# Hybrid decoder trunk: upper and lower weight parts share one tile, at places that depend on the block

## The chip, the cores and the metric

The kernel runs on one core of a Trainium2 chip. The metric is the device time of one execution in microseconds; lower is better. The time before is 1538.71 us, the median of three runs (1538.29 to 1539.51).

## The reference

One decoder layer over 256 tokens, with 16 learned meta tokens in front, in float32 with D_MODEL = 2048. Two branches are computed from one normalised input, gated, summed and projected; a squared-ReLU MLP follows.

```python
h = concatenate([meta, x], axis=1)                       # 272 columns
proj = rmsnorm(h, norm_mix_g) @ w_in                     # fq fk fv ff gq gk gv gr ga gate_fox gate_gla
o_fox = forgetting_attention(fq, fk, fv, ff, b_forget)   # 8 heads of 128
o_gla = gated_linear_attention(gq, gk, gv, g_log)        # 4 heads, keys 256, values 512
y = sigmoid(gate_fox) * (o_fox @ w_o_fox) + sigmoid(gate_gla) * (o_gla @ w_o_gla)
h = h + y @ w_out
h = h + square(relu(rmsnorm(h, norm_mlp_g) @ w_ff1)) @ w_ff2      # D_FF = 8192
return rmsnorm(h, final_norm_g)[:, N_META:]
```

## The kernel before

**How a product is made.** Activations lie transposed: 128 channels on the partitions, tokens along the row. A float32 value is held as an upper part, rounded to the type float32r that TensorE reads at full speed, and a lower part, the remainder. A product takes three terms: upper weights by upper and by lower activations, and lower weights by upper activations.

All weights stand in one DRAM array, w_all, in the order of their use (`stream()`): 272 blocks of 128 output channels by 2048 inputs. A block comes in two halves of 8 k-tiles (`weight_half`, L108). For each half SP issues one DMA of 512 KB into a tile raw (L118). ACT casts it to the upper part, whi (L120), and DVE subtracts to get the lower part, wlo (L121). Before, whi and wlo are two tags of the pool wp, each with five buffers of 4096 bytes a partition; raw has five too. The cast into a buffer waits until TensorE has read what stood in it.

**Two kinds of block.** `gemm2` (L154) serves blocks that need the 256 real tokens alone. For each of 16 k-tiles, mac2 issues one matmul with 512 columns (L143: upper weights by the upper and lower activations at once) and one with 256 (L144: lower weights by upper activations). Its result is evacuated by `total` or `add_residual`: ACT copies half the bank into a tile evb, and DVE adds. `gemm_all` (L163) serves the keys and values, which need the meta tokens too. For each k-tile, mac3 issues three matmuls with 272 columns: L148 (upper weights, lower activations x_lo), L150 (lower weights, x_hi) and L152 (upper weights, x_hi). There are 39 such blocks: 23 in the four GLA heads, 16 in the eight FoX heads. `join` and one DVE product evacuate them. The first seven blocks are computed while h still arrives (`first_weights`), and the small columns (`small`, L386) have weights of their own. Before every matmul TensorE loads its 128 columns of weights, while the matmul before is still reading its moving operand.

**How the moving operand is read.** `steps` (L135) views a row as (i a e) with a = e = 4 and has it read in the order a, i, e: four neighbouring elements (16 bytes), then 64 bytes on, until the row's end, and then again from the next 16 bytes.

**Where things lie.** x (L240) has rows of 576 elements, 2304 bytes or 9 times 256, and its data begin 16 elements into the tile. The other operands (og, y, x2, a) begin 32 elements into theirs (`operand`, L231), with k-tiles 2048 bytes apart; the weights of successive k-tiles are 512 bytes apart. In the built program every whi and wlo buffer begins 128 bytes past a multiple of 256. x_hi begins at 128 and x_lo at 192, and x, og, y, x2, a and of, as gemm2 reads them, at 192. So the moving operand stands 64 bytes from the weights in all 512/256 pairs, and in the 272s 64 (L148) or 0 (L150 and L152), modulo 256.

**Order.** Each engine's instructions are ordered by the tile framework's scheduler, which works from a timeline of its own; a changed wait or buffer can move neighbours past each other. Small work of the heads (scores, transposes, some of them fp32 matmuls) is put between blocks by `later`.

Of the kernel before, what the change touches and what calls it, by code (L numbers as in the profile page):

```python
# [7 lines left out]
F32 = mybir.dt.float32  # L8
F32R = mybir.dt.float32r
# [7 lines left out]
P = 128  # L17
D = 2048
KT = D // P
NM = 16  # L20
NT = 256
NA = NM + NT
EPS = 1e-6
FOX_H, FOX_D = 8, 128
# [8 lines left out]
NL = 4  # L33
# [32 lines left out]
def trunk(ctx: ExitStack, tc: tile.TileContext, hT, w_small, w_all, consts, w_alpha2, out):  # L66
# [3 lines left out]
    def nm(s):  # L70
        serial[0] += 1
        return f"{s}_{serial[0]}"

    const = ctx.enter_context(tc.tile_pool(name="const", bufs=1))
    keep = ctx.enter_context(tc.tile_pool(name="keep", bufs=1))
    wp = ctx.enter_context(tc.tile_pool(name="wp", bufs=5))
    tmp = ctx.enter_context(tc.tile_pool(name="tmp", bufs=2))
# [27 lines left out]
    chunk = [0]  # L105
    HK = KT // 2

    def weight_half(c, i, hi=None):  # L108

        raw = wp.tile([P, HK * P], F32, tag="raw", name=nm("raw"), bufs=RAW)  # L110
        if hi is None:
            hi = wp.tile([P, HK, P], F32R, tag="whi", name=nm("whi"))
        lo = wp.tile([P, HK, P], F32R, tag="wlo", name=nm("wlo"))

        def step(k0, n):
            k = slice(k0, k0 + n)
            cols = slice(k0 * P, (k0 + n) * P)
            nc.sync.dma_start(raw[:, cols], w_all[c][:, i * HK * P + cols.start : i * HK * P + cols.stop])  # L118
            r = raw.rearrange("p (k m) -> p k m", m=P)[:, k, :]
            nc.scalar.copy(hi[:, k, :], r)  # L120
            nc.vector.tensor_tensor(lo[:, k, :], r, hi[:, k, :].bitcast(F32), op=ALU.subtract)  # L121

        return hi, lo, step

    def next_weights(keep_hi=None):
        c = chunk[0]
        chunk[0] += 1
        parts = []
        for i in range(2):
            hi, lo, step = weight_half(c, i, None if keep_hi is None else keep_hi[:, HK * i : HK * (i + 1), :])  # L130
            step(0, HK)
            parts.append((hi, lo))
        return lambda k: (parts[k // HK][0][:, k % HK, :], parts[k // HK][1][:, k % HK, :])
# [43 lines left out]

    def total(ps, t=None):

        b = tmp.tile([P, NT], F32, tag="evb", name=nm("evb"))  # L180
        nc.scalar.copy(b, ps[:, NT:512])  # L181
        if t is None:
            t = tmp.tile([P, NT], F32, tag="evt", name=nm("evt"), bufs=4)
        nc.vector.tensor_tensor(t, ps[:, 0:NT], b, op=ALU.add)  # L184
        return t
# [45 lines left out]
    def operand(pool, name, nk=KT, at=0, **kw):  # L231

        t = pool.tile([P, at + nk * 2 * NT], F32R, name=nm(name), **kw)
        return t[:, at:].rearrange("p (k o t) -> p k o t", o=2, t=NT)
# [2 lines left out]
    h = keep.tile([P, KT, NA + 3], F32, name="h")  # L237

    ROW = 576
    x_row = keep.tile([P, 16 + KT * ROW + 48], F32R, tag="s1", name="x")[:, 16 : 16 + KT * ROW].rearrange(  # L240
        "p (k r) -> p k r", r=ROW)[:, :, 0 : 2 * NA]
    x_hi, x_lo = x_row[:, :, 0:NA], x_row[:, :, NA:]
    x = x_row[:, :, NM : NM + 2 * NT].rearrange("p k (o t) -> p k o t", t=NT)
# [33 lines left out]
    meta = take(KT, NM)  # L277

    def first_weights(c0, n, k0):
        raw = wp.tile([P, HK * P], F32, tag="raw", name=nm("raw"), bufs=RAW)  # L280
        hi = wp.tile([P, HK, P], F32R, tag="whi", name=nm("whi"))
        lo = wp.tile([P, HK, P], F32R, tag="wlo", name=nm("wlo"))
        r, hi, lo = (t[:, 0 : 2 * n * P].rearrange("p (c k m) -> p c k m", k=2, m=P)
                     for t in (raw, hi.rearrange("p k m -> p (k m)"), lo.rearrange("p k m -> p (k m)")))

        def load(c, m):
            return nc.sync.dma_start(r[:, c : c + m], w_all[c0 + c : c0 + c + m, :, k0 * P : (k0 + 2) * P].rearrange(
                "c p (k m) -> p c k m", m=P))

        def cut(c, m, ks=slice(0, 2)):  # L290
            cs = slice(c, c + m)
            i = nc.scalar.copy(hi[:, cs, ks], r[:, cs, ks])
            nc.vector.tensor_tensor(lo[:, cs, ks], r[:, cs, ks], hi[:, cs, ks].bitcast(F32), op=ALU.subtract)
            return i.ins

        return hi, lo, load, cut
# [31 lines left out]
    for s in range(KT // 2):  # L328
# [5 lines left out]
        for kk in range(2):  # L334
            k = 2 * s + kk
# [49 lines left out]

    small = []  # L386
    for i in range(2):
        w = wp.tile([P, HK, P], F32R, tag="whi", name=nm("whi"))
        nc.gpsimd.memset(w.bitcast(F32), 0.0)
        ws = wsm[:, HK * i : HK * (i + 1), :]  # L390
        nc.scalar.copy(w[:, :, 0:40], ws)
        nc.vector.tensor_tensor(w[:, :, 64:104], ws, w[:, :, 0:40].bitcast(F32), op=ALU.subtract)
        small.append(w)
# [71 lines left out]
    og_box = []  # L465

    def og_tile():
        if not og_box:
            og_box.append(operand(keep, "og", at=32, tag="s2"))
        return og_box[0]  # L470

    def gla_gates(ts):
# [30 lines left out]
    def gla_head(hd, sg, ready=None):  # L503
# [11 lines left out]
        def keys(i, ps):  # L515
            def four(ap):
                return ap.rearrange("p (g s t) -> p g s t", g=2, s=2)

            nc.vector.tensor_tensor(kx[:, i].rearrange("p g (s t) -> p g s t", t=C)[:, :, 0:3:2, :],
                                    four(ps[:, 0 : 4 * C]), four(en[:, i, 0 : 4 * C]), op=ALU.mult)  # L520
            nc.vector.tensor_tensor(kz[:, i], *(ap.unsqueeze(1).to_broadcast([P, 4, NB])
                                                for ap in (ps[:, 4 * C : NA], en[:, i, 4 * C :])), op=ALU.mult)

        if ready:
            ps = gemm_all(next_weights())
            keys(0, ready[1])
            keys(1, ps)
        else:
            for i in range(2):
                keys(i, gemm_all(next_weights()))  # L530
        for i in range(2):
            t = ready[0][:, i, :] if ready else total(gemm2(next_weights(), x))
            for q, n, at in ((0, Q1, 0), (Q1, Q3, NT)):
# [59 lines left out]
                nc.scalar.copy(vz, p2)  # L593

        for i in range(4):
            ps = gemm_all(next_weights())
            vT = tmp.tile([P, NA], F32, tag="vT", name=nm("vT"))
            nc.vector.tensor_tensor(vT, ps[:, 0:NA], rb, op=ALU.mult)
            nc.gpsimd.tensor_copy(vg[:, NB * i : NB * (i + 1)], vT[:, 4 * C :])
            later(1, lambda i=i, vT=vT: turn(i, vT))  # L600
# [57 lines left out]
    ps = bank(pg, "psa")  # L658
# [31 lines left out]
    cum.close()  # L690
    branches = ExitStack()
    late = branches.enter_context(tc.tile_pool(name="late", bufs=1, reuse_waits="tile"))
    of = operand(late, "of", FOX_H, at=0)
    negc = late.tile([P, FOX_H, NA], F32, name="negc")
    nc.gpsimd.dma_start(negc.rearrange("p h t -> p (h t)"), fdram.to_broadcast([P, FOX_H * NA]))
    fox = ExitStack()
# [16 lines left out]
    def fox_head(hd):  # L713
        fk = att.tile([P, NA], F32, tag="fk", name=nm("fk"))
        fq = att.tile([P, NT], F32, tag="fq", name=nm("fq"))
        ps = gemm_all(next_weights())
        nc.vector.tensor_tensor(fk, ps[:, 0:NA], rb, op=ALU.mult)
        t = total(gemm2(next_weights(), x))
        nc.vector.scalar_tensor_tensor(fq, t, FOX_D ** -0.5, rbt, op0=ALU.mult, op1=ALU.mult)
# [28 lines left out]
                nc.vector.tensor_scalar(pp, pp, st[:, 4 + b : 5 + b], None, op0=ALU.mult)  # L748

        later(1, scores)  # L750
        ps = gemm_all(next_weights())
        vT = tmp.tile([P, NA], F32, tag="vT", name=nm("vT"))
        nc.vector.tensor_tensor(vT, ps[:, 0:NA], rb, op=ALU.mult)
        va, pa = [], []
# [79 lines left out]
    for j0 in range(0, KT, 2):  # L834
# [5 lines left out]
        for j in range(2):  # L840
            t = total(gemm2(next_weights(), og))
            nc.vector.tensor_tensor(t, gates[2 * j + 1], t, op=ALU.mult)
            nc.vector.tensor_tensor(yf[:, j0 + j, :], gates[2 * j], t, op=ALU.add)
    y = operand(keep, "y", at=32, tag="s1")
    for j in range(KT):
        split_to(y[:, j, 0, :], y[:, j, 1, :], yf[:, j, :])
    mix.close()
# [3 lines left out]


    ht = h[:, :, NM:NA]
    x2 = operand(keep, "x2", at=32, tag="s2")

    def square_sum(j, acc):
        if j == 0:
# [4 lines left out]
            nc.gpsimd.tensor_tensor(acc, acc, sq, op=ALU.add)  # L862

    def add_residual(j, ps):
        b = tmp.tile([P, NT], F32, tag="evb", name=nm("evb"))
        nc.scalar.copy(b, ps[:, NT:512])
        nc.vector.tensor_tensor(ht[:, j, :], ps[:, 0:NT], ht[:, j, :], op=ALU.add)
        nc.vector.tensor_tensor(ht[:, j, :], ht[:, j, :], b, op=ALU.add)
# [22 lines left out]

    acc = gat.tile([P, NT], F32, tag="acc", name="acc3", bufs=1)
    for g in range(NG):
        a = operand(keep, "a", at=32, tag="s1")
        held = []
        for f in range(KT):
            ps = gemm2(next_weights(), x2, pool=px if g == 0 and f < 3 else pg)
            if g == 0 and f == 0:
                held.append(ps)
                continue  # L900
            if g == 0 and f == 1:
                relu2(a, 0, held.pop())
            relu2(a, f, ps)
        last = g == NG - 1
        for j in range(KT - NL if last else KT):
            add_residual(j, gemm2(next_weights(), a))
            if last:
                square_sum(j, acc)
                nc.scalar.activation(ht[:, j, :], ht[:, j, :], AF.Identity, scale=gain(2, j))
                if j == 0:  # L910
                    tc.keep_in_program_order(nc.scalar.preload_act_table_set("natural_log_exp_and_others"))


    whi = keep.tile([P, 48 + NL * KT * P + 16], F32R, tag="s2", name="whi_last")[:, 48 : 48 + NL * KT * P].rearrange(
        "p (n k m) -> p n k m", k=KT, m=P)
    ends = []
    for n in range(NL):
# [150 lines left out]
```

## Time and profile before

| | |
|---|---|
| median of 3 runs | 1538.71 us |
| the profiled execution | 1538.62 us, span 1536.8 us |
| granted TensorE clock | 0.999 |
| DVE busy / ACT busy | 1059.5 us (69%) / 789.6 us (51%) |
| DMA, mean over the span | 191 GB/s |

Four stretches follow each other, in us from the span's start: the first seven blocks (to 44), the GLA heads (to about 330), the FoX heads and first gates (to about 580), then branch projections, output projection and MLP (to the end). In a group's row stand line, engine, operation, output and inputs, shapes and count; then busy time, the mean ns of one, the idle time ahead, and what ended it. In a row of the timeline the first number is the start and the second the duration, in us. In a row of waits stand who waited for whom, us in total, times, and the longest. A matmul's duration runs until its results have left the array and so overlaps the next one's; the spacing of starts is what the stream costs.

### The profile page before, as it was taken

How to read it: one execution, taken by the hardware profiler on the slowest of the kernel's cores; microseconds unless marked ns; L12 is line 12 of the kernel's file. 1: busy time of each engine (PE TensorE's matmuls, PEld its weight loads, DVE VectorE, ACT ScalarE, POOL GpSimd, SP SyncE). 2: the span in 40 equal slices, each digit the busy share in tenths (PEclk: the TensorE clock that was granted, in tenths of full speed). 3: DMA queues.
4: the chain of work that ended last, by engine and by line, in shares of the span. 5: the costliest groups of instructions: out<-in, count | busy, mean ns of one | idle time of the engine just before them, and what ended most of it. 6: DMA issues, size and time to landing. Idle time of an engine off the chain costs nothing.

```text
span 1536.8 us, 25427 instructions
## 1 busy us (share of the span) xinstructions
PE 1525.6 (99%) x9812; PEld 1402.4 (91%) x9812; DVE 1059.5 (69%) x1659; ACT 789.6 (51%) x1271; POOL 127.6 (8%) x213
## 2 busy tenths in 40 slices
PE   9999999999999999999999999999999999999997
PEld 8999999999999999999999899999999999999997
DVE  7898858586666656556777876567765776667765
ACT  6766444555545444444655554445444454444563
POOL 6012000011100000000011000000000000000022
PEclk9999999999999999999999999999999999999999
DMA  9455545465555655666565556666565666656652
GB/s 325 165 165 165 182 161 188 157 210 173 167 166 182 201 195 199 197 198 200 182 212 195 193 195 201 195 200 196 194 202 196 201 196 197 199 195 201 192 192 101
DMA packets 86602, 293.09 MB, mean 191 GB/s; under 512 B 9112, under 2 KB 16800, under 8 KB 86352
## 3 DMA queue, kind: packets, MB, share of 16 engines
q1 hardware_dynamic: 85872, 289.62, 57.6%
q8 instruction: 77, 1.26, 0.3%
q0 software_dynamic: 176, 1.12, 0.2%
q10 hardware_dynamic: 432, 0.72, 0.1%
q14 instruction: 45, 0.37, 0.1%
HBM read 289.32 MB, written 2.11 MB: 190 GB/s over the span
## 4 chain that ended last, share of the span: by engine, by line
PE 97%; DVE 1%; ACT 1%; issue 0%; POOL 0%; DMA 0%; POOLq 0%; ACTq 0%; DVEq 0%
PE ps L143 51%; PE ps L144 26%; PE psa L152 5%; PE psa L148 5%; PE psa L150 4%; PE ps L359 1%; PE ps L361 1%; PE ps L937 1%; PE pa L557 1%; PE ps L921 0%; DVE wlo L121 0%; ACT whi L120 0%; PE po L620 0%; DMA h<-hT_dram 0%; POOL o L985 0%
## 5 line engine op out<-in xcount | busy, mean ns | idle before, releaser
L121 DVE TENSOR_TENSOR wlo<-raw,whi 128x1024 fp32r<-128x1024 f32 x522 | 640.3, 1227 | 400.0 <-ACT whi L120 390.8
L120 ACT CAST whi<-raw 128x1024 fp32r<-128x1024 f32 x522 | 546.9, 1048 | 604.7 <-PE ps L143 534.0
L143 PE MATMUL ps<-x,whi 128*128 128x512 f32 x1952 | 656.4, 382 | 0.8 <-DVE x L874 0.8
L144 PE MATMUL ps<-x,wlo 128*128 128x256 f32 x1952 | 535.3, 274 | 0.0
L143 PEld LDWEIGHTS ps<-x,whi 128*128 128x128 f32 x1952 | 366.4, 188 | 64.2 <-DVE x L874 1.1
L144 PEld LDWEIGHTS ps<-x,wlo 128*128 128x128 f32 x1952 | 366.4, 188 | 0.1
L143 PE MATMUL ps<-a,whi 128*128 128x512 f32 x960 | 320.0, 380 | 0.0
L144 PE MATMUL ps<-a,wlo 128*128 128x256 f32 x960 | 262.4, 274 | 0.0
L143 PEld LDWEIGHTS ps<-a,whi 128*128 128x128 f32 x960 | 179.9, 188 | 30.8
L148 PE MATMUL psa<-x,whi 128*128 128x272 f32 x640 | 182.5, 286 | 0.0
L152 PE MATMUL psa<-x,whi 128*128 128x272 f32 x640 | 180.8, 283 | 0.0
L144 PEld LDWEIGHTS ps<-a,wlo 128*128 128x128 f32 x960 | 180.2, 188 | 0.3
L150 PE MATMUL psa<-x,wlo 128*128 128x272 f32 x624 | 176.3, 283 | 0.0
L148 PEld LDWEIGHTS psa<-x,whi 128*128 128x128 f32 x640 | 120.0, 187 | 0.3
L152 PEld LDWEIGHTS psa<-x,whi 128*128 128x128 f32 x640 | 120.0, 187 | 0.0
L150 PEld LDWEIGHTS psa<-x,wlo 128*128 128x128 f32 x624 | 117.2, 188 | 0.0
L862 POOL TENSOR_TENSOR acc<-acc,hsq 128x256 f32<-128x256 f32 x26 | 28.4, 1092 | 736.4 <-ACT hsq L861 736.4
L143 PE MATMUL ps<-og,whi 128*128 128x512 f32 x256 | 85.8, 380 | 0.0
L143 PE MATMUL ps<-y,whi 128*128 128x512 f32 x256 | 85.3, 380 | 0.0
L144 PE MATMUL ps<-og,wlo 128*128 128x256 f32 x256 | 70.2, 274 | 0.0
L144 PE MATMUL ps<-y,wlo 128*128 128x256 f32 x256 | 70.0, 274 | 0.0
L184 DVE TENSOR_TENSOR evt<-ps,evb 128x256 f32<-128x256 f32 x158 | 65.9, 417 | 0.5 <-ACT evb L181 0.5
(297 smaller groups left out, 1420.9 us busy)
## 6 DMA issues: line engine op xcount, KB each, us to landing
raw<-w_all_dram SPq DMA_DIRECT2D x537, 512.0 KB, 4.3
raw<-w_all_dram SPq DMA_DIRECT2D x8, 384.0 KB, 6.7
h<-hT_dram SPq DMA_DIRECT2D x8, 275.0 KB, 6.8
negc<-fdram POOLq DMA_DIRECT2D x1, 1088.0 KB, 7.9
out_dram<-o SPq DMA_DIRECT2D x2, 512.0 KB, 2.6
raw<-w_all_dram SPq DMA_DIRECT2D x2, 256.0 KB, 3.7
room<-w_small_dram SPq DMA_DIRECT2D x1, 320.0 KB, 7.9
out_dram<-o ACTq DMA_DIRECT2D x1, 320.0 KB, 3.0
```

The costliest lines, as they stand in the source:

```text
L120: nc.scalar.copy(hi[:, k, :], r)
L121: nc.vector.tensor_tensor(lo[:, k, :], r, hi[:, k, :].bitcast(F32), op=ALU.subtract)
L143: nc.tensor.matmul(steps(ps), hi, steps(row(x)), start=first, stop=False)
L144: nc.tensor.matmul(steps(ps[:, 0:NT]), lo, steps(x[:, 0, :]), start=False, stop=last)
L148: nc.tensor.matmul(steps(ps[:, X_LO]), hi, steps(x_lo[:, k]), start=first, stop=False, skip_group_check=True)
L150: nc.tensor.matmul(steps(ps[:, 0:NA]), lo, steps(x_hi[:, k]), start=False, stop=last and hi is None, skip_group_check=True)
L152: nc.tensor.matmul(steps(ps[:, 0:NA]), hi, steps(x_hi[:, k]), start=False, stop=last, skip_group_check=True)
L184: nc.vector.tensor_tensor(t, ps[:, 0:NT], b, op=ALU.add)
L359: nc.tensor.matmul(steps(ps), hi, steps(row(x[:, k])), start=st, stop=False)
L361: nc.tensor.matmul(steps(ps[:, 0:NT]), lo, steps(x[:, k, 0]), start=False, stop=sp)
L557: nc.tensor.matmul(dst, k[:, a], q[:, a, :], start=(a == 0), stop=(a == 1))
L862: nc.gpsimd.tensor_tensor(acc, acc, sq, op=ALU.add)
```

## The change

The two tags whi and wlo become one tag w, of 2 x 1024 + 64 elements (8448 bytes, 33 times 256) with five buffers. A new function `pair` gives the two views. For a block without meta tokens the upper part begins at element 24 and the lower part 24 past the end of the upper one's 1024; for one with meta tokens (`meta=True`: keys, values, and the small columns) they begin at 0 and at 1024 + 20. To make room, evb has one buffer in place of two, and x loses its leading 16 elements. The offsets of the other operands move along, so that the 512/256 pairs keep their distance of 64 bytes.

```diff
+    def pair(meta=False):
+        n = HK * P
+        w = wp.tile([P, 2 * n + 64], F32R, tag="w", name=nm("w"))
+        a, b = (0, 20) if meta else (24, 24)
+        return [w[:, at : at + n].rearrange("p (k m) -> p k m", m=P) for at in (a, n + b)]
+
-    def weight_half(c, i, hi=None):
+    def weight_half(c, i, hi=None, meta=False):
         raw = wp.tile([P, HK * P], F32, tag="raw", name=nm("raw"), bufs=RAW)
+        upper, lo = pair(meta)
         if hi is None:
-            hi = wp.tile([P, HK, P], F32R, tag="whi", name=nm("whi"))
-        lo = wp.tile([P, HK, P], F32R, tag="wlo", name=nm("wlo"))
+            hi = upper
...
-        b = tmp.tile([P, NT], F32, tag="evb", name=nm("evb"))
+        b = tmp.tile([P, NT], F32, tag="evb", name=nm("evb"), bufs=1)
...
-    x_row = keep.tile([P, 16 + KT * ROW + 48], F32R, tag="s1", name="x")[:, 16 : 16 + KT * ROW].rearrange(
+    x_row = keep.tile([P, 0 + KT * ROW + 24], F32R, tag="s1", name="x")[:, 0 : 0 + KT * ROW].rearrange(
...
-        w = wp.tile([P, HK, P], F32R, tag="whi", name=nm("whi"))
+        w = pair(meta=True)[0]
...
-            og_box.append(operand(keep, "og", at=32, tag="s2"))
+            og_box.append(operand(keep, "og", at=56, tag="s2"))
...
-            ps = gemm_all(next_weights())
+            ps = gemm_all(next_weights(meta=True))
...
-    of = operand(late, "of", FOX_H, at=0)
+    of = operand(late, "of", FOX_H, at=24)
...
-    y = operand(keep, "y", at=32, tag="s1")
+    y = operand(keep, "y", at=16, tag="s1")
...
-    x2 = operand(keep, "x2", at=32, tag="s2")
+    x2 = operand(keep, "x2", at=56, tag="s2")
...
-        a = operand(keep, "a", at=32, tag="s1")
+        a = operand(keep, "a", at=16, tag="s1")
...
-    whi = keep.tile([P, 48 + NL * KT * P + 16], F32R, tag="s2", name="whi_last")[:, 48 : 48 + NL * KT * P].rearrange(
+    whi = keep.tile([P, 8 + NL * KT * P + 56], F32R, tag="s2", name="whi_last")[:, 8 : 8 + NL * KT * P].rearrange(
```

All gemm_all calls of the heads get `meta=True`; `add_residual` gets the same `bufs=1`, and `first_weights` takes its tiles from `pair()`.

In the built program x_hi now begins 64 bytes past a multiple of 256 and x_lo at 128. The weights of a block with meta tokens begin at 224 (upper) and 48 (lower): x_hi stands 96 bytes from the upper and 16 from the lower ones. Against the weights that are loaded while a matmul runs, which are the next matmul's, the distances are 80 (behind L148), 96 (L150) and 96 (L152). Weights of the other blocks begin at 64, their moving operands at 128.

The single buffer of evb moves instructions at the start of the GLA stretch. On ACT, behind the first seven blocks, six banks are evacuated (ps_85 to ps_90); join is the small copy for a bank with meta tokens. Before:

```order
L120 CAST whi_665<-raw_664 128x1024
L181 COPY evb_563<-ps_85 128x256
L181 COPY evb_567<-ps_86 128x256
L181 COPY evb_571<-ps_87 128x256
L120 CAST whi_671<-raw_670 128x1024
L181 COPY evb_575<-ps_88 128x256
L181 COPY evb_580<-ps_89 128x256
L120 CAST whi_772<-raw_771 128x1024
L175 COPY join_560<-ps_91 128x16
L181 COPY evb_583<-ps_90 128x256
```

And now:

```order
L126 CAST w_649<-raw_648 128x1024
L187 COPY evb_547<-ps_85 128x256
L126 CAST w_654<-raw_653 128x1024
L187 COPY evb_551<-ps_86 128x256
L181 COPY join_544<-ps_91 128x16
L126 CAST w_754<-raw_753 128x1024
L187 COPY evb_555<-ps_87 128x256
L126 CAST w_759<-raw_758 128x1024
L187 COPY evb_559<-ps_88 128x256
L181 COPY join_622<-psa_570 128x16
L126 CAST w_819<-raw_818 128x1024
L187 COPY evb_564<-ps_89 128x256
```

The copies no longer stand two and three in a row: a cast stands between any two, and the fifth bank (ps_89) is copied behind the fifth cast of this list in place of the second.

On PE, in the second block of values of the first GLA head, the two matmuls of the decays (pz) stand between the 272s. Before:

```order
L148 MATMUL psa_850<-x,whi_845 128x4x17x4
L422 MATMUL pz_728<-ga,csh_730 128x272
L422 MATMUL pz_729<-ga,csh_730 128x272
L150 MATMUL psa_850<-x,wlo_846 128x4x17x4
L152 MATMUL psa_850<-x,whi_845 128x4x17x4
L148 MATMUL psa_850<-x,whi_845 128x4x17x4
L150 MATMUL psa_850<-x,wlo_846 128x4x17x4
L152 MATMUL psa_850<-x,whi_845 128x4x17x4
L586 MATMUL p_112_902<-cons,vT_835 128x128
```

And now:

```order
L154 MATMUL psa_828<-x,w_824 128x4x17x4
L156 MATMUL psa_828<-x,w_824 128x4x17x4
L427 MATMUL pz_710<-ga,csh_712 128x272
L427 MATMUL pz_711<-ga,csh_712 128x272
L158 MATMUL psa_828<-x,w_824 128x4x17x4
L591 MATMUL p_90_880<-cons,vT_815 128x128
```

They moved four 272s later. The other moves on PE are of this kind: the order of blocks and the number of switches between fp32 and float32r matmuls (69) stay. SP's order of loads does not change.

More of the change, by code (lines that the diff above doesn't have):

```diff
@@ L123, in weight_half, with next_weights @@
         return hi, lo, step
-    def next_weights(keep_hi=None):
+    def next_weights(keep_hi=None, meta=False):
         c = chunk[0]
@@ L129, in next_weights @@
         for i in range(2):
-            hi, lo, step = weight_half(c, i, None if keep_hi is None else keep_hi[:, HK * i : HK * (i + 1), :])
+            hi, lo, step = weight_half(c, i, None if keep_hi is None else keep_hi[:, HK * i : HK * (i + 1), :], meta)
             step(0, HK)
@@ L280, in first_weights @@
         raw = wp.tile([P, HK * P], F32, tag="raw", name=nm("raw"), bufs=RAW)
-        hi = wp.tile([P, HK, P], F32R, tag="whi", name=nm("whi"))
-        lo = wp.tile([P, HK, P], F32R, tag="wlo", name=nm("wlo"))
+        hi, lo = pair()
         r, hi, lo = (t[:, 0 : 2 * n * P].rearrange("p (c k m) -> p c k m", k=2, m=P)
@@ L529, in gla_head @@
             for i in range(2):
-                keys(i, gemm_all(next_weights()))
+                keys(i, gemm_all(next_weights(meta=True)))
         for i in range(2):
@@ L595, in gla_head @@
         for i in range(4):
-            ps = gemm_all(next_weights())
+            ps = gemm_all(next_weights(meta=True))
             vT = tmp.tile([P, NA], F32, tag="vT", name=nm("vT"))
@@ L715, in fox_head @@
         fq = att.tile([P, NT], F32, tag="fq", name=nm("fq"))
-        ps = gemm_all(next_weights())
+        ps = gemm_all(next_weights(meta=True))
         nc.vector.tensor_tensor(fk, ps[:, 0:NA], rb, op=ALU.mult)
@@ L750, in fox_head @@
         later(1, scores)
-        ps = gemm_all(next_weights())
+        ps = gemm_all(next_weights(meta=True))
         vT = tmp.tile([P, NA], F32, tag="vT", name=nm("vT"))
@@ L864, in add_residual @@
     def add_residual(j, ps):
-        b = tmp.tile([P, NT], F32, tag="evb", name=nm("evb"))
+        b = tmp.tile([P, NT], F32, tag="evb", name=nm("evb"), bufs=1)
         nc.scalar.copy(b, ps[:, NT:512])
```

## The prediction

> **What bounds the kernel now.** I read the page's busy times, the chain of waits, and who PE waited for.
>
> ```profile
> PE 1525.6 (99%) x9812; PEld 1402.4 (91%) x9812; DVE 1059.5 (69%) x1659; ACT 789.6 (51%) x1271; POOL 127.6 (8%) x213
> PE 97%; DVE 1%; ACT 1%; issue 0%; POOL 0%; DMA 0%; POOLq 0%; ACTq 0%; DVEq 0%
> PE warm L323 <- DVE ones L208: 1.3, 1, 1.3
> PE ps L143 <- DVE x L874: 0.8, 1, 0.8
> PE pn L961 <- ACT sq L942: 0.7, 1, 0.7
> ```
>
> TensorE is busy 99% of the span and is 97% of the chain; its longest total wait for another engine is 1.3 us. So a change pays or costs only by the spacing of matmuls, or by making PE wait where it does not now.
>
> A matmul's shown duration overlaps the next one's, so the spacing has to be read from starts. First the 512/256 pairs of mac2 in the MLP stretch, from the timeline:
>
> ```profile
> 999.66 0.38 PE L143 MATMUL ps<-a,whi 128*128 128x512 f32 x1
> 999.88 0.27 PE L144 MATMUL ps<-a,wlo 128*128 128x256 f32 x1
> 999.99 0.38 PE L143 MATMUL ps<-a,whi 128*128 128x512 f32 x1
> ...
> 1000.99 0.38 PE L143 MATMUL ps<-a,whi 128*128 128x512 f32 x1
> ```
>
> Four pairs take 1.33 us, 333 ns each: 0.22 after a 512, 0.11 after a 256. The difference, 107 ns for 256 columns, is 0.417 ns a column. A 512 is then 213.3 + about 6.7 ns, a 256 is 106.7 + 6.7. By the same line a 272 should be spaced 113.3 + 6.7 = 120.0 ns.
>
> Next two blocks of 48 of mac3's 272-column matmuls, by the start of the first and of the instruction after the last:
>
> ```profile
> 54.94 0.28 PE L148 MATMUL psa<-x,whi 128*128 128x272 f32 x1
> ...
> 60.70 0.28 PE L148 MATMUL psa<-x,whi 128*128 128x272 f32 x1
> ...
> 165.26 0.29 PE L148 MATMUL psa<-x,whi 128*128 128x272 f32 x1
> ...
> 171.14 0.38 PE L143 MATMUL ps<-x,whi 128*128 128x512 f32 x1
> ```
>
> The first takes 5.76 us, 120.0 ns each. The second does the same work with no wait in 5.88 us, 122.5 ns each. So the 272s have a regular state, at just the spacing that the pairs suggest, and an irregular one, 2.5 ns slower. Durations show the same. Here are the groups of the window 55.1 to 60.5, of the window 165.4 to 171.0, and of the whole run:
>
> ```profile
> L148 PE MATMUL psa<-x,whi 128*128 128x272 f32 x16 | 4.5, 281 | 0.0
> L150 PE MATMUL psa<-x,wlo 128*128 128x272 f32 x16 | 4.5, 280 | 0.0
> ...
> L152 PE MATMUL psa<-x,whi 128*128 128x272 f32 x16 | 4.5, 284 | 0.0
> L148 PE MATMUL psa<-x,whi 128*128 128x272 f32 x16 | 4.5, 284 | 0.0
> L150 PE MATMUL psa<-x,wlo 128*128 128x272 f32 x16 | 4.5, 283 | 0.0
> ...
> L148 PE MATMUL psa<-x,whi 128*128 128x272 f32 x640 | 182.5, 286 | 0.0
> L152 PE MATMUL psa<-x,whi 128*128 128x272 f32 x640 | 180.8, 283 | 0.0
> L150 PE MATMUL psa<-x,wlo 128*128 128x272 f32 x624 | 176.3, 283 | 0.0
> ```
>
> Regular is 280.7 on the mean, irregular 283.7, the whole run 284.0. A 272 that starts behind an fp32 matmul is longer for that reason alone:
>
> ```profile
> 326.80 0.41 PE L736 MATMUL pq<-fk,fq 128*128 128x144 f32 x2
> 326.95 0.37 PE L148 MATMUL psa<-x,whi 128*128 128x272 f32 x1
> ```
>
> It lasts 0.37 in place of 0.28, and the program has 27 such places. They account for 27 x 90 / 1904 = 1.3 ns of the mean, which leaves 282.7. So (282.7 - 280.7) / (283.7 - 280.7), two thirds of the 272s, run irregularly. Weights 512 bytes and rows of x 2304 bytes apart repeat their places modulo 256 at every k. The slow pattern is therefore no matter of one k: it is a state that PE falls into and carries along.
>
> **The change, part by part.**
>
> *The places of the 272s' weights.* The count of matmuls, their shapes and their operands stay. What changes is where the moving operand stands from the weights that are loaded beneath it, modulo 256 bytes: 64, 0 and 0 become 80, 96 and 96 (behind L148, L150, L152), for 39 blocks x 48 = 1872 matmuls. All the 512/256 pairs stay at 64. If the new places always give the regular state, the gain is 2/3 x 2.5 ns x 1872 = **3.1 us**. The bounds: the columns alone need 113.3 ns, and the present mean is 120.0 + 2/3 x 2.5 = 121.7, so at the very best 8.4 ns x 1872 = 15.7 us are gained. On the other side the nearest rows are 272s whose moving operand stands 128 or 192 bytes from the next weights, in a FoX head:
>
> ```profile
> L201 PE MATMUL pq<-fksh,fqsh 128*128 128x272 f32 x8 | 2.3, 289 | 0.0
> L202 PE MATMUL pq<-fksl,fqsh 128*128 128x272 f32 x8 | 2.3, 288 | 0.0
> L203 PE MATMUL pq<-fksh,fqsl 128*128 128x272 f32 x8 | 2.3, 288 | 0.0
> ```
>
> They last 288.3, which is 5.6 over the present 282.7; all 1872 at that would lose 10.5 us. Between these ends I take 120.0 ns, because a third of the blocks reaches it now and every pair of the MLP stretch sits on the same line of columns plus 6.7 ns. Both ends stay in the range.
>
> Here the Trainium skill speaks against the change. "TensorE: Matmul & The Clock Gate", Part 2, step by step, says that PE has two independent SBUF read ports and that loading the next tile's weights "doesn't steal SBUF read bandwidth from the running matmul". By that rule the place of the weights is worth nothing, and the sum would be the present time. The trace agrees where it shows pairs at exactly 333 ns for hundreds of microseconds. It does not explain 120.0 beside 122.5 ns for the same shapes with the same waits.
>
> *The pairs that use x.* Their places are kept, but they start from the state that the 272s leave. Right after the irregular block above, from the timeline, and then the whole run's groups:
>
> ```profile
> 171.82 0.39 PE L143 MATMUL ps<-x,whi 128*128 128x512 f32 x1
> ...
> 172.84 0.39 PE L143 MATMUL ps<-x,whi 128*128 128x512 f32 x1
> ...
> L143 PE MATMUL ps<-x,whi 128*128 128x512 f32 x1952 | 656.4, 382 | 0.8 <-DVE x L874 0.8
> L143 PE MATMUL ps<-a,whi 128*128 128x512 f32 x960 | 320.0, 380 | 0.0
> ```
>
> Three pairs in 1.02 us are 340 ns each, 6.7 more than in the MLP. The group with x (which holds x2's 1024 pairs too, since a name's number is left out) has 382 for 380: 2 x 1952 = 3.9 us at most, of which some 21 starts behind fp32 matmuls, at 0.09 us, take 1.9. Of the other 2.0 us I take half, **1.0 us**, as gained; none or all is as possible.
>
> *One buffer for evb.* ACT's copy now waits until DVE has added the one before.
>
> ```profile
> L181 ACT COPY evb<-ps 128x256 f32<-128x256 f32 x160 | 58.4, 365 | 1.4 <-DVE evt L184 1.3
> L184 DVE TENSOR_TENSOR evt<-ps,evb 128x256 f32<-128x256 f32 x158 | 65.9, 417 | 0.5 <-ACT evb L181 0.5
> L121 DVE TENSOR_TENSOR wlo<-raw,whi 128x1024 fp32r<-128x1024 f32 x522 | 640.3, 1227 | 400.0 <-ACT whi L120 390.8
> L120 ACT CAST whi<-raw 128x1024 fp32r<-128x1024 f32 x522 | 546.9, 1048 | 604.7 <-PE ps L143 534.0
> ```
>
> A block of 16 pairs lasts 5.3 us and a half block 2.7, while copy, one subtraction ahead on DVE and the add are 0.37 + 1.23 + 0.42 = 2.0 us. PE's own stream hides that. Were the cover gone, 236 evacuations (160 and add_residual's 76) would stand behind an add of 0.42 us each, 99 us. Only at the start do six totals stand in a row. There each copy now waits for an add which stands behind a subtraction, and behind the copies on ACT stand the casts of the next weights; PE waits for those. The six need 6 x 2.0 = 12 us at worst, and PE has the small block and the first key and value blocks, some 15 us (45.2 to 60.7 in the timeline), to do meanwhile; the bank that each block takes comes from one total each. I take **0.2 us** lost, up to 2.
>
> *Upper and lower in one tile.* The cast into a tile now waits for the last lower product too, 0.11 to 0.12 us later than the upper one in a half of 2.7 us. ACT already spends 534 us waiting for PE to free a buffer, with four more halves ready, some 10.7 us of work. If that cover were gone PE would wait for cast and subtraction, 2.3 us a half. Cost nothing. SP issues the same loads in the same order, and the few PE instructions that changed place keep their neighbours' kinds: no more switches between fp32 and fp32r than before (69). I take nothing for them, 1 us either way.
>
> *Sum.* 3.1 + 1.0 - 0.2 = 3.9 us, against the profiled execution's 1538.62 us (span 1536.8 and 1.8 around it), which is 0.09 under the median of the runs shown. 1538.6 - 3.9 = **1534.7 us**.
>
> **The rivals.**
>
> *The new places are better than the regular state.* Half of the 6.7 ns over the columns goes too: another 3.3 ns x 1872 = 6.2 us, 1528.5 us. For it: that remainder is no part of the columns. Against it: no stretch of hundreds of 272s or 256s holds a smaller spacing.
>
> *Nothing is gained.* 64 to 96 bytes or 0 to 80 leave the mix of the two states, or the spacing has nothing to do with places: 1538.6 us, or up to 1 us beside it. For it: the regular and the irregular blocks before have the very same places. Against it: the pairs, which differ only in shape and place, hold one state over the whole MLP.
>
> *Slower: the new places collide more.* The mechanism is that the 272s run as those of pq, 288.3 long: 1538.6 + 10.5 = 1549 us. With the pairs in x thrown into the 340 ns state as well (928 pairs x 6.7 ns, some 6 us, less the part there now) it ends near 1553. It decides from the point where the 272s' mean, freed of the starts behind fp32, exceeds 282.7 ns. For it: an odd multiple of 16 bytes is tried nowhere before, and pq shows that other places can cost 8 ns. Against it: pq's operands are read in one run, mac3's in steps of 64 bytes.
>
> **How the numbers follow.** Forecast 0.45, better than regular 0.12, no change 0.15, slower by collisions 0.28. The likeliest gives 1534.7 us, by itself 1532.5 to 1537. Of the forecast about a tenth lies within 0.2% (3.1 us, about what a measurement of this kernel can tell from no change), the other three cases fall on their own sides: faster 0.52, same 0.20, slower 0.28. The range that leaves two in ten out reaches from the better case, 1528, up into the collisions, 1548.
>
> **What would show it.** Right: the 272s' three groups near 281 to 282 (with the fp32 starts), blocks of 48 in 5.76 us, x's 512s nearer to 380, the MLP's pairs still at 333 ns, and PE's waits for other engines as now. Wrong: 272s at 285 or more; x's pairs mostly at 340; a wait of PE for ACT's cast between 45 and 62 us, which would put the loss on evb; or the MLP's pairs off 333 ns, which would mean that the common tile moved more than the 272s.

## The result and the profile after

The changed kernel takes 1535.41 us (median, 1534.76 to 1535.73), the kernel before 1538.92 us (1538.24 to 1539.66) on the same chip. The ratio is 0.9977, 95% interval 0.9968 to 0.9985: 3.5 us faster. The profiled spans, 1536.8 and 1533.5 us, differ by 3.3 us.

From the page of the kernel after, the busy times and the chain of waits:

```profile
PE 1522.7 (99%) x9812; PEld 1399.6 (91%) x9812; DVE 1073.3 (70%) x1659; ACT 795.3 (52%) x1271; POOL 128.8 (8%) x213
PE 97%; DVE 1%; ACT 1%; issue 0%; DMA 0%; POOL 0%; SPq 0%; POOLq 0%; DVEq 0%; ACTq 0%
```

The bound is the same, and PE is busy 2.9 us less with as many matmuls. Whom PE waited for: a row of the kernel before that belongs to the first seven blocks, then the kernel after:

```profile
PE ps L359 <- ACT whi L292: 0.4, 1, 0.4
...
PE warm L328 <- DVE ones L214: 1.3, 1, 1.3
PE ps L364 <- ACT w L297: 0.7, 2, 0.6
PE pn L966 <- ACT sq L947: 0.7, 1, 0.7
```

The wait for x2 (0.8 us before) has gone. In the first seven blocks PE waits for a cast twice, 0.7 us in all, where it waited once, 0.4 us. The costliest groups of the kernel after:

```profile
L126 ACT CAST w<-raw 128x1024 fp32r<-128x1024 f32 x522 | 547.2, 1048 | 278.1 <-PE ps L150 211.5
L149 PE MATMUL ps<-x,w 128*128 128x512 f32 x1952 | 656.3, 382 | 0.0
...
L149 PE MATMUL ps<-a,w 128*128 128x512 f32 x960 | 320.2, 380 | 0.0
...
L154 PE MATMUL psa<-x,w 128*128 128x272 f32 x640 | 182.0, 285 | 0.0
...
L158 PE MATMUL psa<-x,w 128*128 128x272 f32 x640 | 179.7, 282 | 0.0
L156 PE MATMUL psa<-x,w 128*128 128x272 f32 x624 | 176.0, 282 | 0.0
L187 ACT COPY evb<-ps 128x256 f32<-128x256 f32 x160 | 59.6, 372 | 207.7 <-PE ps L150 206.1
```

The three groups of 272s last 182.0 + 179.7 + 176.0 = 537.7 us together, before 539.6. x's 512s stay at 382 ns. On ACT, evb's copies now wait 207.7 us, nearly all of it for PE, where they waited 1.4; the casts wait 278.1 in place of 604.7. That second difference was not foreseen, and it turns out to matter.

**Where the time went.** In both traces I took the spacing of each matmul's start from the next, less the regular (columns + 16) / 2.4 ns (120.0 for 272, 220.0 for 512, 113.3 for 256). Sums of what is left, where it is under 16 ns (the larger gaps are switches from and to fp32 matmuls and waits):

| us over the regular spacing | before | after |
|---|---|---|
| 272s (1872 intervals) | 3.21 | 0.92 |
| x's pairs right behind a block of 272s (173 and 174) | 0.48 | 0.05 |
| x's pairs behind fp32 matmuls (902 and 910) | 1.30 | 1.96 |

Together with PE's gap before x2 this is -2.3 for the 272s, +0.2 for x's pairs (-0.4 and +0.7), and -1.0 for x2: 3.1 of the 3.3 us of the spans. The first of the 272s behind the first seven blocks starts 0.4 us earlier (at 44.83 us, before at 45.23), which is about the rest; the gaps beside fp32 matmuls I did not follow. The last row of the table also holds pairs of the first seven blocks and some behind small float32r matmuls.

The timeline of PE in the kernel after, over the two GLA blocks that took 5.88 us each before and the pairs behind them:

```profile
158.91 0.28 PE L154 MATMUL psa<-x,w 128*128 128x272 f32 x1
...
164.67 0.28 PE L154 MATMUL psa<-x,w 128*128 128x272 f32 x1
...
170.44 0.39 PE L149 MATMUL ps<-x,w 128*128 128x512 f32 x1
...
171.45 0.38 PE L149 MATMUL ps<-x,w 128*128 128x512 f32 x1
...
175.78 0.38 PE L149 MATMUL ps<-x,w 128*128 128x512 f32 x1
```

Both blocks take 5.76 to 5.77 us, 120 ns a matmul, and the three pairs behind them 1.01 us where they took 1.02; the first block of 16 pairs takes 5.34 us, before 5.44 (171.14 to 176.58).

### The profile page after: what moved, and what is told of

It reads as the page before. It is cut to its first block, busy times and chain, and to the rows that moved or that the text cites. A ratio compares the mean times of both kernels' runs of the same rounds, so it can differ in the third digit from the quotient of the medians.

```text
span 1533.5 us, 25365 instructions
## 1 busy us (share of the span) xinstructions
PE 1522.7 (99%) x9812; PEld 1399.6 (91%) x9812; DVE 1073.3 (70%) x1659; ACT 795.3 (52%) x1271; POOL 128.8 (8%) x213
## 4 chain that ended last, share of the span: by engine, by line
PE 97%; DVE 1%; ACT 1%; issue 0%; DMA 0%; POOL 0%; SPq 0%; POOLq 0%; DVEq 0%; ACTq 0%
PE ps L149 51%; PE ps L150 26%; PE psa L154 5%; PE psa L158 5%; PE psa L156 4%; PE ps L364 1%; PE ps L942 1%; PE ps L366 1%; PE pa L562 1%; PE ps L926 0%; DMA raw<-w_all_dram 0%; PE po L625 0%; DVE w L127 0%; ACT w L126 0%; POOL o L990 0%
## 5 line engine op out<-in xcount | busy, mean ns | idle before, releaser
L127 DVE TENSOR_TENSOR w<-raw,w 128x1024 fp32r<-128x1024 f32 x522 | 645.9, 1237 | 260.2 <-ACT w L126 251.0
L126 ACT CAST w<-raw 128x1024 fp32r<-128x1024 f32 x522 | 547.2, 1048 | 278.1 <-PE ps L150 211.5
L149 PE MATMUL ps<-x,w 128*128 128x512 f32 x1952 | 656.3, 382 | 0.0
L150 PE MATMUL ps<-x,w 128*128 128x256 f32 x1952 | 535.7, 274 | 0.0
L149 PEld LDWEIGHTS ps<-x,w 128*128 128x128 f32 x1952 | 366.4, 188 | 63.2
L150 PEld LDWEIGHTS ps<-x,w 128*128 128x128 f32 x1952 | 366.4, 188 | 0.2
L149 PE MATMUL ps<-a,w 128*128 128x512 f32 x960 | 320.2, 380 | 0.0
L150 PE MATMUL ps<-a,w 128*128 128x256 f32 x960 | 263.0, 274 | 0.0
L149 PEld LDWEIGHTS ps<-a,w 128*128 128x128 f32 x960 | 180.2, 188 | 31.0
L154 PE MATMUL psa<-x,w 128*128 128x272 f32 x640 | 182.0, 285 | 0.0
L150 PEld LDWEIGHTS ps<-a,w 128*128 128x128 f32 x960 | 180.2, 188 | 0.0
L158 PE MATMUL psa<-x,w 128*128 128x272 f32 x640 | 179.7, 282 | 0.0
L156 PE MATMUL psa<-x,w 128*128 128x272 f32 x624 | 176.0, 282 | 0.0
L187 ACT COPY evb<-ps 128x256 f32<-128x256 f32 x160 | 59.6, 372 | 207.7 <-PE ps L150 206.1
L154 PEld LDWEIGHTS psa<-x,w 128*128 128x128 f32 x640 | 120.2, 188 | 0.3
L158 PEld LDWEIGHTS psa<-x,w 128*128 128x128 f32 x640 | 120.2, 188 | 0.1
L156 PEld LDWEIGHTS psa<-x,w 128*128 128x128 f32 x624 | 117.4, 188 | 0.0
```

Source lines behind the costliest of these rows:

```text
L149: nc.tensor.matmul(steps(ps), hi, steps(row(x)), start=first, stop=False)
L150: nc.tensor.matmul(steps(ps[:, 0:NT]), lo, steps(x[:, 0, :]), start=False, stop=last)
L154: nc.tensor.matmul(steps(ps[:, X_LO]), hi, steps(x_lo[:, k]), start=first, stop=False, skip_group_check=True)
L156: nc.tensor.matmul(steps(ps[:, 0:NA]), lo, steps(x_hi[:, k]), start=False, stop=last and hi is None, skip_group_check=True)
L158: nc.tensor.matmul(steps(ps[:, 0:NA]), hi, steps(x_hi[:, k]), start=False, stop=last, skip_group_check=True)
```

## The experiments

Every run stands beside runs of the kernel before on its chip (1538.92 us beside the change, 1538.1 to 1538.4 beside the others). "Gain" is this difference of medians, negative for faster; an interval of the ratio is about 0.0009, or 1.4 us, to either side. "272s over" is the first row of the table above for that kernel. In the traces of the ten runs with the common tile (the change, e2 and all the others but e1 and e12) PE, ACT, DVE and POOL each have the very same instructions in the same order, so that these differ in the places of weights and in nothing else.

| kernel | 272s: distance behind L154, L156, L158 | time, us | gain, us | 272s over, us |
|---|---|---|---|---|
| before | 64, 0, 0 | | 0 | 3.21 |
| after | 80, 96, 96 | 1535.41 | -3.51 | 0.92 |
| e1: evb alone | 64, 0, 0 | 1538.42 | +0.16 | 3.08 |
| e2: old places | 64, 0, 0 | 1537.28 | -0.98 | 3.22 |
| e5: upper part only | 64, 96, 96 | 1538.12 | -0.15 | 3.84 |
| e6: all 96 | 96, 96, 96 | 1538.57 | +0.30 | 4.65 |
| e3: shift by 64 | 16, 32, 32 | 1538.43 | +0.17 | 4.91 |
| e8: all 80 | 80, 80, 80 | 1538.74 | +0.47 | 5.16 |
| e4: shift by 128 | 208, 224, 224 | 1539.45 | +1.19 | 6.18 |
| e12: rings in step | 64, 0, 0 | 1538.30 | +0.21 | 3.17 |

### The change taken apart

The kernel before with the single evb buffer alone:

```diff
-        b = tmp.tile([P, NT], F32, tag="evb", name=nm("evb"))
+        b = tmp.tile([P, NT], F32, tag="evb", name=nm("evb"), bufs=1)
```

in `total` and in `add_residual`.

> The kernel before with one buffer for evb and nothing else; the places of the 272s' weights stay at 64, 0 and 0 bytes. Theory P (the places make the gain, through the spacing of the 272s): the 272s keep the mix, spacing 121.7 ns, so their 2.3 us stay; only what the new order of instructions brings (the 1.0 us wait for x2 near 846 us, about 0.5 us at the start) can go: 1537.4 to 1538.9. Rival S (the scheduler's new order makes the gain): 1535.4, as the whole change.

And the changed kernel with the common tile and the single evb, but the old distances for all blocks (both parts 24 elements behind the start of their half, at 24 and 1024 + 24):

```diff
-        a, b = (0, 20) if meta else (24, 24)
+        a, b = (24, 24)
```

> The changed kernel with the weights of the blocks with meta tokens at 24 and 24 as all others, so that the 272s stand 64, 0 and 0 bytes from the next weights as before; common tile and one evb stay. Theory P: the mix of the two states is back, the 272s' spacing is 121 to 122 ns, 1537 to 1538. Rival S: 1535.4, and the 272s' spacing does not matter. Rival T (common tile as such): 1535.4 too, with 120 ns spacing.

Measured: 1538.42 against 1538.26 us (ratio 1.0001, 0.9992 to 1.0010) and 1537.28 against the same (0.9992, 0.9984 to 1.0001). Whom PE waited for, with evb alone and then with the old places:

```profile
PE ps L143 <- DVE x L874: 0.8, 1, 0.8
```

```profile
PE warm L328 <- DVE ones L214: 1.3, 1, 1.3
PE pn L966 <- ACT sq L947: 0.7, 1, 0.7
```

Theory P came out in both runs. Rivals S (1535.4 us in both) and T (1535.4 us in the second) fall.

The single evb leaves x2's wait where it was and costs nothing that can be measured. The common tile takes the wait away, whatever the places. It also makes most of the new order: in the trace of e1 the first copies into evb are parted by casts on ACT, but the two matmuls pz stand one place later on PE, not four, and ACT's copies do not wait for PE. The copies with evb alone, then with the old places:

```profile
L181 ACT COPY evb<-ps 128x256 f32<-128x256 f32 x160 | 58.7, 367 | 4.5 <-DVE evt L184 3.8 <-DVE qd L184 0.7
...
L187 ACT COPY evb<-ps 128x256 f32<-128x256 f32 x160 | 59.6, 373 | 207.5 <-PE ps L150 205.8 <-DVE r2b L235 1.6
```

So the moves on PE that the section on the change puts down to evb come in the main with the common tile. The 272s with the old places, from the groups of e2:

```profile
L154 PE MATMUL psa<-x,w 128*128 128x272 f32 x640 | 182.3, 286 | 0.0
L158 PE MATMUL psa<-x,w 128*128 128x272 f32 x640 | 180.8, 283 | 0.0
L156 PE MATMUL psa<-x,w 128*128 128x272 f32 x624 | 176.5, 283 | 0.0
```

Their sum is 539.6 us again, as before. The kernel after differs from this one in two offsets only, and its 272s are 1.9 us shorter by the groups, 2.3 by the starts, its span 2.3 us. So about 2.3 to 2.5 of the 3.5 us are the places, and about 1.0 the common tile. Of the latter the median's interval by itself still holds zero; the wait that is missing in the trace is what carries it.

The kernel before and e2 also tell a distance from a place: from the one to the other the weights and the moving operand of the 272s both moved by 64 bytes, and at the same distances the excess is the same, 3.21 and 3.22 us. Weights that move by 64 bytes alone change it (e3 below).

### Which distances are the good ones

Both weights moved by the same amount, by 64 and by 128 bytes:

```diff
-        a, b = (0, 20) if meta else (24, 24)
+        a, b = (16, 36) if meta else (24, 24)
```

> The changed kernel with both weight parts of the blocks with meta tokens 64 bytes later: the 272s stand 16, 32 and 32 bytes from the next weights in place of 80, 96 and 96. Theory P64 (only the place within 64 bytes counts): the same as the change, 120 ns after some ten matmuls, 1535.4 within 0.5. Rival P128 or P256 (distance modulo 128 or 256 counts): another spacing, anything from 119 to 128 ns, that is 1534 to 1549.

```diff
-        a, b = (0, 20) if meta else (24, 24)
+        a, b = (32, 52) if meta else (24, 24)
```

> The changed kernel with both weight parts of the blocks with meta tokens 128 bytes later: distances 208, 224 and 224 in place of 80, 96 and 96. P64 and P128: the same as the change, 1535.4 within 0.5. P256: another spacing of the 272s, 1534 to 1549.

Both lost the whole gain of the places. From the costliest groups of the kernel shifted by 128:

```profile
L154 PE MATMUL psa<-x,w 128*128 128x272 f32 x640 | 184.0, 289 | 0.0
L158 PE MATMUL psa<-x,w 128*128 128x272 f32 x640 | 182.0, 285 | 0.0
L156 PE MATMUL psa<-x,w 128*128 128x272 f32 x624 | 177.2, 284 | 0.0
```

The sum is 543.2 us, 5.5 more than in the kernel after. Had only the distance modulo 64 or modulo 128 counted, one or both of these would have run as the kernel after. So neither 64 nor 128 bytes is a period of the effect; a period of 256 or more wasn't tried. The distance is given to the next weights, which are loaded beneath the matmul. Moving the weights moves the distance to the matmul's own weights too, and no run here tells the two apart.

Three more ask whether 16 bytes matter, and which of the three distances does the work:

```diff
-        a, b = (0, 20) if meta else (24, 24)
+        a, b = (0, 24) if meta else (24, 24)
```

> The changed kernel with the lower weights of the blocks with meta tokens 16 bytes later: distances behind the three matmuls 64, 96 and 96 in place of 80, 96 and 96. If the upper weights' 96 does the work: excess of the 272s over 120 ns some 0.9 us in all as in the change, 1535.4 within 0.4. If the lower weights' 80 is needed as well: excess 3 us or more, 1537 to 1539.

```diff
-        a, b = (0, 20) if meta else (24, 24)
+        a, b = (0, 16) if meta else (24, 24)
```

> The changed kernel with the lower weights of those blocks 16 bytes earlier: distances 96, 96 and 96. Smooth dependence on the place (neighbours alike): 1535.4 within 0.5. Each 16 bytes on its own: excess of the 272s anywhere from 0.5 to 6 us, 1535 to 1540.5.

```diff
-        a, b = (0, 20) if meta else (24, 24)
+        a, b = (4, 20) if meta else (24, 24)
```

> The changed kernel with the upper weights of those blocks 16 bytes later: distances 80, 80 and 80 in place of 80, 96 and 96. Smooth dependence: 1535.4 within 0.5. Each 16 bytes on its own: excess of the 272s anywhere from 0.5 to 6 us, 1535 to 1540.5.

None of them comes near the change. 16 bytes to either side in the first distance cost 2.9 and 3.7 us in the 272s' starts (64 or 96 for 80), 16 bytes in the other two 4.2 us (80 for 96). A rule of the kind "96 is good" or "80 is good" falls: it is the set 80, 96, 96 that is good. Only seven of the many sets have been seen (the six of these kernels and the one before), so that others as good or better may exist.

### The pairs that use x

Four more places for the weights of x's pairs, on top of the change. The 272s keep 80, 96 and 96. In each, `next_weights()` of the four `gemm2(..., x)` calls gets `meta="x"`; the pair of offsets differs:

```diff
-        a, b = (0, 20) if meta else (24, 24)
+        a, b = (16, 20) if meta == "x" else (0, 20) if meta else (24, 24)
```

(80 behind a 512, 96 behind a 256)

> The changed kernel in which the 512/256 pairs that read x, too, get other places: 80 behind the 512 and 96 behind the 256, in place of 64 and 64. If 80/96 is a better pair of places for any shape: the 2.1 us of excess of x's pairs fall under 0.7, 1534.0. If 64 is right for pairs and each shape has places of its own: the pairs lose their 333 ns and the time grows, by 919 pairs x 3 to 15 ns, to 1538 to 1549.

and with `(56, 56)` (192 behind both), `(28, 28)` (48) and `(40, 40)` (0):

> The changed kernel in which the 512/256 pairs that read x stand 192 bytes from the next weights in place of 64; the 272s stay as in the change. If pairs depend on the place modulo 256, as the 272s do: the excess of x's pairs leaves 2.1 us, to anywhere from 0.5 (1533.8) to 8 us (1541.5). If modulo 128 is enough for pairs: 1535.4 within 0.4.

> The same with x's pairs at 48 bytes. If each 16 bytes counts for pairs too: an excess other than 2.1 us, 1533.8 to 1541.5. If pairs keep their two states at any place near 64: 1535.4 within 0.4.

> The same with x's pairs at 0 bytes. If pairs depend on the place modulo 64 alone: 1535.4 within 0.4. If not: 1533.8 to 1541.5, and below 1535 it would beat both kernels.

| distance behind 512 / 256 | time, us | gain, us | x's pairs over the regular spacing, us |
|---|---|---|---|
| 64 / 64 (the change) | 1535.41 | -3.51 | 2.1 |
| 192 / 192 | 1537.54 | -0.82 | 4.4 |
| 48 / 48 | 1537.60 | -0.76 | 4.2 |
| 80 / 96 | 1539.07 | +0.80 | 5.9 |
| 0 / 0 | 1540.74 | +2.38 | 7.3 |

The last column counts what is left under 25 ns, where the table of the result stops at 16: with 0 / 0, 84 intervals lie between. So counted, the four lie 2.3, 2.1, 3.8 and 5.2 us over the change, and their times 2.1, 2.2, 3.7 and 5.3. The 272s stay at 0.9 to 1.0 us over.

From the costliest groups of the kernel with 0 / 0:

```profile
L149 PE MATMUL ps<-x,w 128*128 128x512 f32 x1952 | 661.1, 384 | 0.0
L150 PE MATMUL ps<-x,w 128*128 128x256 f32 x1952 | 535.7, 274 | 0.0
```

The 512s take 4.8 us more than in the kernel after (656.3). So the place matters to these too, 64 is the best of the five, and the set that is good for the 272s is bad for the pairs. With 192 the 256s fall short of 113.3 ns (0.96 us below the regular spacing in all), but the 512s stand 5.3 us over theirs: the 113.3 ns are no floor of a 256. Of all versions run, none was faster than the change.

### x2's wait

One run asked whether the wait for x2 came from the two rings of weight buffers being out of step in the kernel before (the small columns take whi buffers but no wlo):

```diff
     for i in range(2):
         w = wp.tile([P, HK, P], F32R, tag="whi", name=nm("whi"))
+        wp.tile([P, HK, P], F32R, tag="wlo", name=nm("wlo"))
```

> The kernel before, with one tile of the tag wlo taken and left unused for every half block of small columns, so that the two rings of buffers stay in step as those of the common tile do; places, evb and all instructions stay. Theory R (PE's wait of 0.8 us for the first half of x2 comes from the rings being out of step: a cast then waits for a later product than it would in the common tile): the wait for DVE x is gone, the 272s stay at about 3.2 us over their regular spacing, and the time is about 1537.4 us against 1538.4 before. Rival (the wait comes from the evacuation at that place, whatever the rings): the wait stays at 0.8 us and the time at 1538.4 us.

Measured: 1538.30 against 1538.09 us (ratio 1.0001, 0.9992 to 1.0010). Whom PE waited for:

```profile
PE ps L143 <- DVE x L875: 0.8, 1, 0.8
```

The wait stays; theory R falls. What does tell the kernels apart is the order on ACT. Counted in the traces, 286 casts of 128x1024 stand ahead of the copy into evb that x2 hangs on (the 112th) in the kernel before, in e1 and in e12, all of which have the wait; 285 in e2 and in the kernel after, which don't. Ahead of 220 of the 236 copies there is one cast fewer. It is a matter of who goes first at the end of a block. The timelines of PE, ACT and DVE at the last block of the output projection, in the kernel before:

```profile
841.92 0.38 PE L143 MATMUL ps<-x,whi 128*128 128x512 f32 x1
...
847.89 0.49 PE L143 MATMUL ps<-x,whi 128*128 128x512 f32 x1 [0.81 <-DVE x L874]
...
842.00 1.05 ACT L120 CAST whi<-raw 128x1024 fp32r<-128x1024 f32 x1 [0.90 <-PE ps L143]
842.95 0.36 ACT L866 COPY evb<-ps 128x256 f32<-128x256 f32 x1
...
843.08 1.22 DVE L121 TENSOR_TENSOR wlo<-raw,whi 128x1024 fp32r<-128x1024 f32 x1 [0.56 <-ACT whi L120]
844.22 0.42 DVE L867 TENSOR_TENSOR h<-ps,h 128x256 f32<-128x256 f32 x1
844.67 0.43 DVE L868 TENSOR_TENSOR h<-h,evb 128x256 f32<-128x256 f32 x1
845.75 1.22 DVE L121 TENSOR_TENSOR wlo<-raw,whi 128x1024 fp32r<-128x1024 f32 x1 [0.64 <-ACT whi L120]
846.89 0.95 DVE L874 SCALAR_TENSOR_TENSOR x<-h,x 128x256 fp32r<-128x256 f32 x1
```

And in the kernel after:

```profile
839.59 0.38 PE L149 MATMUL ps<-x,w 128*128 128x512 f32 x1
...
844.59 0.38 PE L149 MATMUL ps<-x,w 128*128 128x512 f32 x1
...
839.85 0.37 ACT L871 COPY evb<-ps 128x256 f32<-128x256 f32 x1 [1.67 <-PE ps L150]
840.12 1.05 ACT L126 CAST w<-raw 128x1024 fp32r<-128x1024 f32 x1
...
840.25 0.43 DVE L872 TENSOR_TENSOR h<-ps,h 128x256 f32<-128x256 f32 x1 [0.82 <-ACT evb L871]
840.71 0.43 DVE L873 TENSOR_TENSOR h<-h,evb 128x256 f32<-128x256 f32 x1
841.20 1.23 DVE L127 TENSOR_TENSOR w<-raw,w 128x1024 fp32r<-128x1024 f32 x1
842.34 0.96 DVE L879 SCALAR_TENSOR_TENSOR x<-h,x 128x256 fp32r<-128x256 f32 x1
```

The first row of each is the start of the next block, whose first 15 pairs do not need the k-tile of x2 that this bank makes, and run for 15 x 0.333 = 5.0 us. Before, a cast goes ahead of the copy, so on DVE a subtraction goes ahead of the adds, another one behind them, and x2's last part is done 5.92 us after the block's end (841.92 to 847.84), 0.9 too late. After, the copy goes first, one subtraction is left between, and it is done 3.71 us after (839.59 to 843.30), 1.3 us early.

Why the order turned: before, the cast waits for the last upper product (PE ps L143), which ends ahead of the last lower one that the copy needs. In the common tile it waits for the lower one itself (PE ps L150), as the copy does. That this is what made the scheduler prefer the copy is argued from the waits' names, and wasn't tried by itself. It does so all over the program, as ACT's idle times show; only at x2 does PE wait for the outcome.

## Why the prediction was right, and where not

**The forecast.** 1534.7 us against 1535.41, a gain of 3.9 against 3.5: the sum is right. Two of its terms are not, and a third, not in it, made up for them. That the sum came so near is therefore luck in part: the places alone gave 2.3 to 2.5 us where 4.1 had been put down to them.

**The 272s, -3.1.** Right in the mechanism: between e2 and the kernel after the distance alone takes them from the mix of two states to 120.0 ns, but for the first 8 to 16 of a run. The present excess was right too (2/3 x 2.5 = 1.67 ns a matmul, 1.71 by the starts). The size was off, 2.3 in place of 3.1. The step that was mis-sized is the condition "if the new places always give the regular state". They give it after a few matmuls. Mean ns over 120.0, by the place of a matmul behind the start of its run of 272s:

| 272s that begin behind fp32 matmuls | 1st to 8th | 9th to 16th | 17th to 24th | 25th to 32nd | later |
|---|---|---|---|---|---|
| before | 1.93 | 2.77 | 1.63 | 2.13 | 0.95 |
| after | 2.15 | 0.55 | 0.16 | 0.13 | 0.04 |

The first eight are as slow as ever. These, behind fp32 and float32r alike, make 0.63 of the 0.92 us that stay. One such block in the timeline of the kernel after:

```profile
73.16 0.37 PE L154 MATMUL psa<-x,w 128*128 128x272 f32 x1
73.36 0.29 PE L156 MATMUL psa<-x,w 128*128 128x272 f32 x1
...
75.07 0.28 PE L154 MATMUL psa<-x,w 128*128 128x272 f32 x1
...
78.91 0.28 PE L158 MATMUL psa<-x,w 128*128 128x272 f32 x1
```

From the second to the sixteenth matmul are 14 steps in 1.71 us, 122 ns each; from there to the last 32 steps in 3.84, 120.0 each. The new places do not start regularly; they lead into the regular state and hold it. The old ones could hold it (the block of 5.76 us in the prediction) but were often not led into it. That also answers the rival's argument that regular and irregular blocks had the same places.

**x's pairs, -1.0.** This fell: 382 ns before and after, 0.2 us lost by the starts. The mechanism was right, for the pairs right behind a block of 272s (0.48 us over before, 0.05 after). The step that failed is "they start from the state that the 272s leave": 174 of their intervals do so, while 910 run behind fp32 matmuls, and those went from 1.30 to 1.96. Leaving out the first seven blocks and the pairs behind small float32r matmuls, it is 0.80 us before, 0.82 in e2 and 1.51 in the kernel after, over some 680 intervals each. Since e2 has the same order and the same places of these pairs, it is the places of the 272s that cost this 0.7 us, though fp32 matmuls stand between. It comes by whole blocks and both ways: the 32 intervals that begin at 285.42 us in the kernel after are 0.11 us over there and 0.02 in e2, and those at 279.73 us are 0.02 and 0.10. How a place acts across the fp32 matmuls stays open. In the kernel after, a block of pairs behind other pairs that began behind fp32:

```profile
102.33 0.39 PE L149 MATMUL ps<-x,w 128*128 128x512 f32 x1
...
103.35 0.39 PE L149 MATMUL ps<-x,w 128*128 128x512 f32 x1
```

Three pairs in 1.02 us, the 340 ns state still. Half of the excess was taken as gained without asking from the trace what stands ahead of each block of pairs, which could have been counted.

**evb, +0.2.** Nothing measured (+0.16 with an interval of 1.4 us to either side), and the cover that was named held.

**The common tile, "cost nothing".** This is the step that was wrong in kind. It looked for a loss, 0.11 us of a later cast behind a cover of 10.7 us, and found none. It did not ask what a later cast does to the instructions behind it on ACT: by the account above, argued and not tried by itself, it lets the evacuation past, and there one of PE's waits hung on the evacuation, the 1.0 us of x2. The row of that wait stood in the prediction's first fence. PE's own moves, taken as nothing, were within the 1 us stated.

**The rule weighed.** The Trainium skill, "TensorE: Matmul & The Clock Gate", Part 2, has it that loading the next weights "doesn't steal SBUF read bandwidth from the running matmul". The prediction read from this that the place of the weights is worth nothing. The runs disagree with that: the kernel after and e2 differ in the place of the weights alone, and in 2.3 us of 272s; e4 and the kernel after in 5.3. Whether bandwidth is what is lost no run here shows.

**The rivals.** Better than regular fell: once led in, the spacing is 120.0 ns and no less. Nothing gained fell, the interval of the ratio ends at 0.9985. Slower by collisions fell for these places, but its mechanism is real: five other sets of distances put the 272s 0.6 to 3.0 us above their old time, none by the 10.5 us that pq's rows suggested. Pq's 288.3 ns were a poor guide to the size.

## What to carry to other kernels

Where a matmul stream bounds the kernel, compare starts with the pace of its best stretch, and try where the weights stand against the moving operand in steps of 16 bytes; neither direction nor size could be foretold, and a set that suits one shape may harm another. When a wait is made later by 0.1 us, look in the built program for what it lets past on its engine, and then for those of the bounding engine's waits, however short, that hang on that. A gain that depends on what runs ahead is worth only the share of instructions that do run behind it, which a trace of before can tell.

## What the runs showed of the hardware

- The distance of the weights from the moving operand of a float32r matmul changes its pace. Steps of 16 bytes count, and neither 64 nor 128 is a period: over 1872 272s by 0.92 to 6.18 us in total, 0.5 to 3.3 ns each, and over x's pairs by 2.1 to 7.3 us.
- The regular pace is (columns + 16) / 2.4 ns in the shapes seen: 120.0 for 272, 333.3 for 512 and 256 together, over hundreds of us. One place (192) took the 256s 0.96 us below it in all, at the 512s' cost.
- The pace is a state that is carried along: 272s after fp32 matmuls need some 8 to 16 matmuls at about 122 ns to reach 120.0, with good places, and pairs behind regular 272s start regularly. What in the chip holds this state no run here shows.
